# Two-layer attention backbone on one core: exponentials left unscaled, gates divided by the row sums, and another order of the first loads

## The chip, the cores and the metric

One core of one Trainium2 chip runs the whole program in one launch. The metric is device time in microseconds (us); less is better. Engines are named as in the profile: PE (matrix multiply, with PEld its weight loads), DVE (vector), ACT (scalar), POOL (GpSimd), SP (issues the DMAs).

## The reference

Two layers over 512 latent tokens (a grid of 8 rows and 64 columns) and 256 context tokens, width 1024. Cut to what matters:

```python
hx = _rmsnorm(x, norm_g) * (1.0 + scale_x) + shift_x       # scale, shift from silu(c) @ w_ada + b_ada
px = hx @ w_in                                              # one projection for everything below
a_k, a_v, b_k, b_v, a_q, b_q, a_z, b_z, g_a, g_b = _split(px, SPLIT_SIZES)
# branch A: 8 heads, neighbourhood window 8 x 16 with a bias, and all context keys
# branch B: 8 query heads on 2 key heads, rotary, all latent and all context keys
p = jax.nn.softmax(s, axis=-1)
a_att = p @ v                                               # the same for b_att
o_a = (a_att * jax.nn.silu(a_z)) @ w_o_a
o_b = (b_att * jax.nn.silu(b_z)) @ w_o_b
merged = jax.nn.sigmoid(g_a) * o_a + jax.nn.sigmoid(g_b) * o_b
x_new = x + gate_x * (merged @ w_out)
```

In layer 0 the context tokens go through the same computation (they read context keys alone); in layer 1 only the latent tokens are updated. All is float32.

## The kernel before

**Products.** Every float32 operand of a product is split into a high and a low part, and each product is three matmuls (`mm3`: high by high, high by low, low by high; lines 345 to 347). Weights come by `load_w` and `load_w2`: a DMA into one of three `raw` tiles, ACT writes the high part `whi` (lines 315, 330), DVE or POOL the low part `wlo` (lines 318, 332).

**Stages of a layer.** The projections for branch A (keys, values, queries); the attention of branch A, called NA below (`na_scores`, `na_values`); the projections for branch B; the attention of branch B, called GQ (`gq_scores`, `gq_values`); then the merge: the two output projections, the sigmoid gates, `w_out` and the residual. The gate projections (`fill_chunks`, `o_chunks`) are cut into pieces and handed out between heads as filler for PE (`run(fill, ...)`).

**One head of attention.** `pipeline` takes the scores of head h, and then the values of head h-1. For each of four blocks of 128 queries PE puts the scores in PSUM, DVE finds the row maximum (line 753 in NA, 899 in GQ), and ACT takes the exponential into a tile `p` with the row sums in `r` (lines 756, 901). Then `softmax_tail` takes the reciprocal of the sums on DVE (line 607) and multiplies `p` with 0.5 and the reciprocal: in blocks 0 and 2 on DVE (line 610), in blocks 1 and 3 on POOL (lines 612 and 613). In layer 0 the context queries are a fifth block (`ctx_scores`, on DVE). The values transpose `p` on PE (lines 621, 623), split it (`pth` on ACT, line 626; `ptl` on DVE, line 627), multiply it with the values, and `head_out` (lines 635 to 637) adds two halves and multiplies the result into the gate tensor `za` or `zb`, which holds z times (1 + tanh(z/2)); the 0.5 makes that silu. The `p` tiles come from a pool of 7 slots in NA of layer 0, 8 in NA of layer 1, and 10 in GQ (`NP_NA`, `NP_GQ`). At the end of GQ `hilo` (lines 519, 520) splits `zb` for the output projection.

**The start of layer 0.** Six tiles of 128 tokens are loaded (`load_x`, line 130); the latent ones are gathered from the grid so that tokens run down the columns:

```python
x_lat = x0.rearrange("(r c) d -> c r d", c=GRID_W)
```

`start_y` normalises a tile and transposes it into `yT`. The modulation's weights come in four parts of 2 MB (`ada_load`: two DMAs `rawx` and `rawy`), each of which serves two of the eight channel blocks k; `ada_part` multiplies them with silu(c) on PE (line 190) and DVE makes scale and shift in `modc` (lines 171 to 173). `start_mods(q)` applies them to two channel blocks of `yT` (line 301), and ACT and DVE or POOL split the result into `hx` (lines 304, 305). Then the first projection (`C_AK`) takes these two blocks for all six token tiles, and so on for q = 0 to 3.

**Order.** The instructions are written in program order and then put in an order per engine by a planner with a model of the times (`schedule_with_timeline_sim=True`); each engine then runs its own list in that order, SP's DMA queue included.

Of the kernel before, what the change touches and what calls it, by code (L numbers as in the profile page):

```python
# [28 lines left out]
NA_POOL = (1, 3)  # L29
GQ_POOL = (1, 3)  # L30
# [17 lines left out]
def hybrid_kernel(es: ExitStack, tc, x, ctx, cvec, w_ada, w_ada0, small, gvec, w_in, w_o_a, w_o_b, w_out,  # L48
# [48 lines left out]

    x0, ctx0 = x[0], ctx[0]
    x_lat = x0.rearrange("(r c) d -> c r d", c=GRID_W)
# [33 lines left out]
    for t in range(6):  # L133
        load_x(t)
# [66 lines left out]
    def ada_steps(l, tiles, halves, nv, pool):  # L201
# [13 lines left out]
        def dot(h, i, v):  # L215
            if v == 0:
                load_tile(h, i)
            w = cb["w"]
            o = w if v == nv - 1 else pool.tile([128, 512], BF16, tag="junk", name=nm("junk"), bufs=1)
            ins = nc.cur_bb.bb.instructions  # L220
            before = next(j for j in reversed(ins) if j.engine == mybir.EngineType.DVE)
            n = len(ins)
            V.tensor_tensor_reduce(o, w, cb[h][:, v, :], 1.0, 0.0, ALU.mult, ALU.add, asum[:, i, h, v:v + 1])
            for j in nc.cur_bb.bb.instructions[n:]:
                if j.engine == mybir.EngineType.DVE:
                    tc.add_manual_dep(j, before.name, mybir.DependencyInfo(
                        mybir.DependencyClass.NoSync, mybir.DependencyReason.DATA), reason="program order")
# [69 lines left out]
    def start_mod(k, yT, hx):  # L297

        d = yT[k // 4].rearrange("p (k n) -> p k n", k=4)[:, k % 4, :]
        for v, (n0, n1) in enumerate(((0, 512), (512, 768))):  # L300
            V.tensor_scalar(d[:, n0:n1], d[:, n0:n1], modc[:, 0, v, 8 + k:9 + k], modc[:, 0, v, k:k + 1],
                            ALU.mult, ALU.add)
        hi, lo = hx_k(hx, 0, k), hx_k(hx, 1, k)
        S.copy(R(hi), d)
        (G if k % 3 == 2 else V).tensor_tensor(R(lo), d, hi, ALU.subtract)
# [65 lines left out]
    def start_mods(q):  # L371
        for k in range(2 * q, 2 * q + 2):
            start_mod(k, yT, hx0)
# [83 lines left out]
    def layer(l, hx, nxt, mid):  # L457
# [146 lines left out]
        if True:  # L604
            def softmax_tail(p, n, r, pieces, eng=None):

                V.reciprocal(r, r)  # L607
                for i, (c0, c1) in enumerate(pieces):
                    if eng is None:
                        V.tensor_scalar(p[:, c0:c1], p[:, c0:c1], r[:, i:i + 1], 0.5, ALU.mult, ALU.mult)  # L610
                    else:
                        G.tensor_scalar(r[:, i:i + 1], r[:, i:i + 1], 0.5, None, ALU.mult)  # L612
                        G.tensor_tensor(p[:, c0:c1], p[:, c0:c1],  # L613
                                        r[:, i:i + 1].to_broadcast([128, c1 - c0]), ALU.mult)
# [63 lines left out]
            def ctx_scores(q, kh, kl):  # L678
# [8 lines left out]
                r = sp.tile([128, 2], F32, tag="r", name=nm("r"), bufs=8)  # L687
                for i in range(2):
                    S.activation(p[:, 256 * i:256 * i + 256], pss[:, 256 * i:256 * i + 256], AF.Exp,
                                 bias=mx[:, i:i + 1], accum_out=r[:, i:i + 1])  # L690
                softmax_tail(p, 512, r, [(0, 256), (256, 512)])
# [41 lines left out]
            def na_scores(h, q, kh, kl):  # L733
                load_bias(h)
                ps_ = []
                for i in range(4):
# [4 lines left out]
                    else:  # L741
# [7 lines left out]
                        for kk, b in ((kh, True), (kl, False)):  # L749
# [5 lines left out]
                    r = sp.tile([128, 2], F32, tag="r", name=nm("r"), bufs=8)  # L755
                    S.activation(p[:, :512], p[:, :512], AF.Exp, bias=mx[:, 0:1], scale=-1.0,
                                 accum_out=r[:, 0:1])
                    softmax_tail(p, 512, r[:, 0:1], [(0, 512)], G if i in NA_POOL else None)
# [33 lines left out]
            def pipeline(fill, spread, scores_of, values_of, last=None, bg=[]):  # L792
# [13 lines left out]
                run(bg, len(bg))  # L806
                values_of(7, prev)
# [4 lines left out]
            def na_first(h):  # L812
# [4 lines left out]
                ps_ = na_scores(h, q, kh, kl)  # L817
                return ps_, ctx_scores(q, kh, kl) if first else None
# [12 lines left out]
            pipeline(fill, 9, na_first, values_of(za, na_values), bg=bg)  # L831
# [59 lines left out]
            def gq_scores(q, kh, kl):  # L891
                ps_ = []
                for i in range(4):
# [6 lines left out]
                    r = sp.tile([128, 2], F32, tag="r", name=nm("r"), bufs=8)  # L900
                    S.activation(p, pss, AF.Exp, bias=mx[:, 0:1], accum_out=r[:, 0:1])
                    softmax_tail(p, 768, r[:, 0:1], [(0, 768)], G if i in GQ_POOL else None)
# [19 lines left out]
            def gq_first(h):  # L922
                kh, kl = gkt[h // 4]
                q = stage_q(qbv[:, h // 2, :], h % 2)
                ps_ = gq_scores(q, kh, kl)
                return ps_, ctx_scores(q, kh, kl) if first else None
# [11 lines left out]
            pipeline(fill, 8, gq_first, values_of(zb, gq_values), early, bg)  # L938
# [149 lines left out]
```

## Time and profile before

| | us |
|---|---|
| median of 3 runs (1182.45 to 1184.28) | 1183.07 |
| profiled execution, time | 1181.47 |
| profiled execution, span | 1179.7 |
| start of layer 0 up to the end of its first projection | about 73 |
| NA, layer 0 and layer 1 | 173.0 and 114.3 |
| GQ, layer 0 and layer 1 | 186.5 and 142.7 |
| share of the span that PE, PEld, DVE, ACT, POOL are busy | 96%, 80%, 69%, 49%, 43% |

The edges of the stages were read from the first and last instructions of their lines. A matmul in the timeline lasts longer than the distance to the next one, because they are pipelined; so PE's busy share counts an engine as full that could have run its matmuls more densely.

### The profile page before, as it was taken

The numbers are of one execution on the slowest core, as the hardware profiler recorded it, in microseconds if no ns is written. First come the engines' busy times: TensorE is split into PE (matmuls) and PEld (weight loads), VectorE is DVE, ScalarE is ACT, GpSimd is POOL, SyncE is SP. The second block draws the span as 40 slices with busy tenths as digits, with TensorE's granted clock in tenths as the row PEclk, the third lists the DMA queues.
The fourth block names the chain that finished last, engine by engine and source line by source line (L and its number), as shares of the span: only waits on it lengthen the run. The fifth ranks groups of instructions, "written<-read, shape, count | busy, mean of one in ns | idle before, by whom it ended". The sixth has DMA issues, their size and how long they took to land. (4 is left out here: it accounts for less than half of the span.)

```text
span 1179.7 us, 17337 instructions
## 1 busy us (share of the span) xinstructions
PE 1130.4 (96%) x6078; PEld 948.8 (80%) x6078; DVE 812.2 (69%) x1506; ACT 575.0 (49%) x1171; POOL 508.3 (43%) x463
## 2 busy tenths in 40 slices
PE   4999999899999999999999999999999999999898
PEld 3688877788897888878788887887888878877686
DVE  4476689987474499978683455339786757798573
ACT  4353255466453355566430355436666545756531
POOL 2362444453267233453420225336553764654311
PEclk9999999999999999999999999999999999999999
DMA  9544323422152343371170322312322525452133
GB/s 315 188 144 135 111 80 111 120 82 61 55 157 87 118 143 112 72 263 38 41 192 18 125 90 72 116 43 88 119 78 71 159 80 183 142 179 98 37 127 96
DMA packets 88128, 134.05 MB, mean 114 GB/s; under 512 B 10756, under 2 KB 52712, under 8 KB 86376
## 3 DMA queue, kind: packets, MB, share of 16 engines
q1 hardware_dynamic: 88040, 132.94, 36.1%
q8 instruction: 48, 0.79, 0.3%
q14 instruction: 40, 0.33, 0.1%
HBM read 115.58 MB, written 17.32 MB: 113 GB/s over the span
## 5 line engine op out<-in xcount | busy, mean ns | idle before, releaser
L627 DVE TENSOR_TENSOR ptl<-pst,pth 128x512 fp32r<-128x512 f32 (+1 forms) x176 | 115.9, 672 | 40.7 <-ACT pth L626 39.6
L332 POOL TENSOR_TENSOR wlo<-raw,whi 128x512 fp32r<-128x512 f32 x64 | 91.7, 1435 | 119.8 <-ACT whi L330 99.6
L345 PE MATMUL psf<-hx,whi 128*128 128x512 f32 (+1 forms) x368 | 138.9, 378 | 1.1 <-DVE za L480 1.0
L346 PE MATMUL psf<-hx,whi 128*128 128x512 f32 (+1 forms) x368 | 138.3, 376 | 0.0
L347 PE MATMUL psf<-hx,wlo 128*128 128x512 f32 (+1 forms) x368 | 137.9, 375 | 0.0
L626 ACT CAST pth<-pst 128x512 fp32r<-128x512 f32 (+1 forms) x176 | 98.8, 578 | 80.0 <-PE pst L623 56.2
L345 PE MATMUL psx<-whi,hx 128*128 128x512 f32 (+1 forms) x368 | 134.9, 374 | 0.0
L346 PE MATMUL psx<-wlo,hx 128*128 128x512 f32 (+1 forms) x368 | 134.4, 369 | 0.0
L347 PE MATMUL psx<-whi,hx 128*128 128x512 f32 (+1 forms) x368 | 133.4, 370 | 0.0
L318 POOL TENSOR_TENSOR wlo<-raw,whi 128x512 fp32r<-128x512 f32 (+1 forms) x52 | 68.1, 1310 | 146.1 <-ACT whi L315 123.6
L315 ACT CAST whi<-raw 128x512 fp32r<-128x512 f32 (+1 forms) x112 | 64.8, 591 | 111.2 <-PE psx L347 39.6
L330 ACT CAST whi<-raw 128x512 fp32r<-128x512 f32 x128 | 78.1, 621 | 56.2 <-DMA raw<-in_w_in_dram 41.0
L623 PE MATMUL pst<-ident,p 128*128 128x128 f32 x640 | 100.4, 273 | 3.6 <-POOL p L613 1.2
L623 PEld LDWEIGHTS pst<-ident,p 128*128 128x128 f32 x640 | 77.8, 140 | 16.8 <-POOL p L613 1.6
L613 POOL TENSOR_TENSOR p<-p,r 128x512 f32<-128x512 f32 (+1 forms) x64 | 86.6, 1353 | 5.2
L332 DVE TENSOR_TENSOR wlo<-raw,whi 128x512 fp32r<-128x512 f32 x64 | 63.4, 991 | 36.0 <-ACT whi L330 35.5
L612 POOL TENSOR_SCALAR r<-r 128x1 f32<-128x1 f32 x64 | 24.2, 378 | 135.9 <-DVE r L607 123.9
L345 PEld LDWEIGHTS psf<-hx,whi 128*128 128x128 f32 x368 | 69.5, 189 | 12.9 <-DVE za L480 1.7
L347 PEld LDWEIGHTS psx<-whi,hx 128*128 128x128 f32 x368 | 69.4, 189 | 12.0 <-issue 0.8
L345 PEld LDWEIGHTS psx<-whi,hx 128*128 128x128 f32 x368 | 70.0, 191 | 11.1
L346 PEld LDWEIGHTS psx<-wlo,hx 128*128 128x128 f32 x368 | 69.6, 189 | 11.3
L347 PEld LDWEIGHTS psf<-hx,wlo 128*128 128x128 f32 x368 | 69.4, 188 | 11.6
(239 smaller groups left out, 3049.4 us busy)
## 6 DMA issues: line engine op xcount, KB each, us to landing
raw<-in_w_in_dram SPq DMA_DIRECT2D x160, 256.0 KB, 2.9
rawb<-in_w_ada_dram SPq DMA_DIRECT2D x64, 256.0 KB, 2.7
gs<-zt SPq DMA_DIRECT2D x32, 256.0 KB, 2.6
raw<-in_w_out_dram SPq DMA_DIRECT2D x32, 256.0 KB, 2.7
tg<-gs SPq DMA_DIRECT2D x4, 1536.0 KB, 7.8
rawx<-in_w_ada_dram SPq DMA_DIRECT2D x4, 1024.0 KB, 11.9
rawy<-in_w_ada_dram SPq DMA_DIRECT2D x4, 1024.0 KB, 12.7
raw<-in_w_o_a_dram SPq DMA_DIRECT2D x16, 256.0 KB, 3.2
```

What stands on the lines that cost most here:

```text
L315: S.copy(hi[:, :n], raw[:, :n])
L318: e.tensor_tensor(lo[:, :n], raw[:, :n], F(hi[:, :n]), ALU.subtract)
L330: S.copy(hi, raw)
L332: lo_eng(i).tensor_tensor(lo, raw, F(hi), ALU.subtract)
L345: T.matmul(ps, lhs[0], rhs[0], start=first, stop=False)
L346: T.matmul(ps, lhs[0], rhs[1], start=False, stop=False)
L347: T.matmul(ps, lhs[1], rhs[0], start=False, stop=last)
L612: G.tensor_scalar(r[:, i:i + 1], r[:, i:i + 1], 0.5, None, ALU.mult)
L613: G.tensor_tensor(p[:, c0:c1], p[:, c0:c1], r[:, i:i + 1].to_broadcast([128, c1 - c0]), ALU.mult)
L623: T.transpose(pt[:, c0:c0 + 128], src, ident)
L626: S.copy(hi[:, n0:n1], pt[:, n0:n1])
L627: V.tensor_tensor(lo[:, n0:n1], pt[:, n0:n1], F(hi[:, n0:n1]), ALU.subtract)
```

## The change

The exponentials are no longer multiplied with anything. The sums of the two heads of a pair, for all query blocks, are kept in one tile `r` of 128 by 12 (8 in layer 1). `invert` doubles them and takes the reciprocal; `sums_out` transposes them on PE into 12 rows of 128, ACT copies these into a `p` tile, and a DMA writes them to DRAM. One head later `normalise` reads them back, each row to 64 partitions, into one or two `p` tiles, and POOL multiplies the pair's channels of `za` or `zb` with them. For the last pair this comes ahead of the values of head 7. `behind` fixes the place of some of these instructions: after what was written before them on the same engine.

At the start, only two token tiles are loaded ahead of the modulation's first part; then come the first two channel blocks of the projection's weights, the other four token tiles, and the modulation's second part. The first two token tiles are normalised ahead of `ada_part(0)`, the other four behind it. `start_mods(0)` works in groups of 256 tokens. The weights of the projection's next part are loaded ahead of the modulation's next part. The host lays x out in column order, so that each token tile is one contiguous piece of DRAM.

```diff
+    rd = [drp.tile([12, 128], F32, name=f"rd{i}") for i in range(4)]
...
         if t < 4:
-            return x_lat[16 * t:16 * t + 16]
+            return x0[128 * t:128 * t + 128, :]
...
-    for t in range(6):
+    for t in range(2):
         load_x(t)
...
-    def start_mod(k, yT, hx):
+    def start_mod(k, yT, hx, cuts):
         d = yT[k // 4].rearrange("p (k n) -> p k n", k=4)[:, k % 4, :]
-        for v, (n0, n1) in enumerate(((0, 512), (512, 768))):
-            V.tensor_scalar(d[:, n0:n1], d[:, n0:n1], modc[:, 0, v, 8 + k:9 + k], modc[:, 0, v, k:k + 1],
-                            ALU.mult, ALU.add)
         hi, lo = hx_k(hx, 0, k), hx_k(hx, 1, k)
-        S.copy(R(hi), d)
-        (G if k % 3 == 2 else V).tensor_tensor(R(lo), d, hi, ALU.subtract)
+        for n0, n1 in zip(cuts, cuts[1:]):
+            for v, (c0, c1) in enumerate(((n0, min(n1, 512)), (max(n0, 512), n1))):
+                if c0 < c1:
+                    V.tensor_scalar(d[:, c0:c1], d[:, c0:c1], modc[:, 0, v, 8 + k:9 + k], modc[:, 0, v, k:k + 1],
+                                    ALU.mult, ALU.add)
+            S.copy(R(hi[:, n0:n1]), d[:, n0:n1])
+            (G if k % 3 == 2 else V).tensor_tensor(R(lo[:, n0:n1]), d[:, n0:n1], hi[:, n0:n1], ALU.subtract)
...
     def start_mods(q):
-        for k in range(2 * q, 2 * q + 2):
-            start_mod(k, yT, hx0)
+        cuts = (0, 256, 512, 768) if q == 0 else (0, 768)
+        for i in range(len(cuts) - 1):
+            for k in range(2 * q, 2 * q + 2):
+                start_mod(k, yT, hx0, cuts[i:i + 2])
...
                 if q == 0:
-                    mid(0)
+                    mid(0, lambda: w.extend(load_w(W, C_AK, 512, 2, mix_lo)))
                 if q < 3:
-                    mid(q + 1)
+                    mid(q + 1, lambda: w.extend(load_w(W, C_AK, 512, 2, mix_lo, 2 * q + 2)))
                 start_mods(q)
-                w += load_w(W, C_AK, 512, 2, mix_lo, 2 * q)
...
+            def invert(r):
+                n = 6 if first else 4
+                V.tensor_scalar(r[:, 0:n], r[:, 0:n], 2.0, None, ALU.mult)
+                V.reciprocal(r[:, 0:n], r[:, 0:n])
+
+            def sums_out(j, r):
+                n = 12 if first else 8
+                pt = psw(128, "t")
+                T.transpose(pt[0:n], r[:, 0:n // 2].rearrange("p j e -> p (j e)"), ident)
+                row = p_tile()[:, 0:128]
+                S.copy(row[0:n], pt[0:n])
+                behind(lambda: nc.sync.dma_start(rd[j][0:n], row[0:n]))
+
+            def normalise(j, z, perm):
+                zv = z.rearrange("p (f n) -> p f n", f=4)[:, j]
+                n = 6 if first else 4
+                w = min(att["w"] // 128, n)
+                for j0 in range(0, n, w):
+                    j1 = min(j0 + w, n)
+                    rb = p_tile()[:, 0:128 * (j1 - j0)]
+                    for e in range(2):
+                        nc.sync.dma_start(rb[64 * e:64 * e + 64].rearrange("p (j q) -> p j q", q=128),
+                                          rd[j].rearrange("(j e) q -> e j q", e=2)[e:e + 1, j0:j1]
+                                          .to_broadcast([64, j1 - j0, 128]))
+                    if perm and j0 == 0:
+                        zp = zv[:, 0:512].rearrange("p (s n) -> p s n", n=64)[:, 0:8:7]
+                        G.tensor_tensor(zp, zp, rb[:, 0:128].rearrange("p (s n) -> p s n", n=64), ALU.mult)
+                        G.tensor_tensor(zv[:, 64:448], zv[:, 64:448], rb[:, 128:512], ALU.mult)
                     else:
-                        G.tensor_scalar(r[:, i:i + 1], r[:, i:i + 1], 0.5, None, ALU.mult)
-                        G.tensor_tensor(p[:, c0:c1], p[:, c0:c1],
-                                        r[:, i:i + 1].to_broadcast([128, c1 - c0]), ALU.mult)
+                        zp = zv[:, 128 * j0:128 * j1]
+                        G.tensor_tensor(zp, zp, rb, ALU.mult)
...
-                    softmax_tail(p, 512, r[:, 0:1], [(0, 512)], G if i in NA_POOL else None)
...
-                    softmax_tail(p, 768, r[:, 0:1], [(0, 768)], G if i in GQ_POOL else None)
...
                     if prev is not None:
                         values_of(h - 1, prev)
+                    if h % 2:
+                        invert(att["r"])
+                        sums_out(h // 2, att["r"])
+                    elif h:
+                        behind(lambda: normalise(h // 2 - 1, z, perm))
...
                 run(bg, len(bg))
+                normalise(3, z, perm)
                 values_of(7, prev)
...
-    def start_part(q):
+    def start_part(q, load):
         if q == 0:
             ada_w[0] = ada_load(0, npool)
-            for t in range(6):
+            load()
+            for t in range(2, 6):
+                load_x(t)
+            ada_w[1] = ada_load(1, npool)
+            for t in range(2):
                 start_y(t, npool, yT)
-        if q < 3:
-            ada_w[q + 1] = ada_load(q + 1, npool)
+        else:
+            load()
+            if q < 3:
+                ada_w[q + 1] = ada_load(q + 1, npool)
         ada_part(q, ada_w.pop(q), npool)
+        if q == 0:
+            for t in range(2, 6):
+                start_y(t, npool, yT)
...
+    d['x'] = d['x'].reshape(1, ROWS, GRID_W, DM).transpose(0, 2, 1, 3).reshape(1, NLAT, DM)
```

More of the change, by code (lines that the diff above doesn't have):

```diff
@@ L96, in psw, with behind @@
         return pool.tile([128, cols], F32, tag=kind, name=nm("ps" + kind))[:, :n]
+    def behind(fn):
+        ins = nc.cur_bb.bb.instructions
+        n, last = len(ins), {}
+        for i in ins[::-1]:
+            last.setdefault(i.engine, i.name)
+            if len(last) == 5:
+                break
+        fn()
+        for i in nc.cur_bb.bb.instructions[n:]:
+            if i.engine in last:
+                tc.add_manual_dep(i, last[i.engine], mybir.DependencyInfo(
+                    mybir.DependencyClass.NoSync, mybir.DependencyReason.DATA), reason="program order")
+            last[i.engine] = i.name
     x0, ctx0 = x[0], ctx[0]
-    x_lat = x0.rearrange("(r c) d -> c r d", c=GRID_W)
     o_lat = out[0].rearrange("(r c) d -> c r d", c=GRID_W)
@@ L219, in dot @@
             o = w if v == nv - 1 else pool.tile([128, 512], BF16, tag="junk", name=nm("junk"), bufs=1)
[L220 to L227, printed above, removed]
+            behind(lambda: V.tensor_tensor_reduce(o, w, cb[h][:, v, :], 1.0, 0.0, ALU.mult, ALU.add,
+                                                  asum[:, i, h, v:v + 1]))
         res = []
@@ L676, in cut, with ctx_scores @@
                 return lambda k: k[:, a:b]
-            def ctx_scores(q, kh, kl):
+            def ctx_scores(q, kh, kl, r, e):
                 pss = ps_score()
```

43 lines of the change are left out of this document (20 added, 23 removed).

## The prediction

> **What bounds the kernel now.** First the page's totals, then the busy time of each engine by stage. The stages, in order: start of layer 0; NA of layer 0; projections for branch B; GQ of layer 0; merge; and from layer 1 projections, NA, GQ. The columns are PE, PEld, DVE, ACT, POOL (instructions in brackets), clock, DMA share, GB/s.
>
> ```profile
> span 1179.7 us, 17337 instructions
> PE 1130.4 (96%) x6078; PEld 948.8 (80%) x6078; DVE 812.2 (69%) x1506; ACT 575.0 (49%) x1171; POOL 508.3 (43%) x463
> ...
> 0.00:73.00 73.00, 56.73 (x282) 40.23 (x283) 34.73 (x71) 32.04 (x54) 22.80 (x29) 0.98 0.69 236
> 158.50:331.50 173.00, 165.71 (x1038) 146.73 (x1039) 139.60 (x309) 95.68 (x220) 75.11 (x68) 1.00 0.30 91
> 331.50:404.50 73.00, 71.04 (x399) 61.00 (x399) 39.58 (x71) 29.43 (x65) 44.66 (x43) 1.00 0.38 116
> 404.50:591.00 186.50, 180.53 (x1092) 156.69 (x1091) 157.08 (x285) 106.50 (x222) 79.83 (x67) 1.00 0.37 112
> 591.00:718.00 127.00, 127.00 (x627) 107.26 (x626) 69.67 (x112) 45.69 (x101) 23.48 (x25) 1.00 0.32 97
> ...
> 800.70:915.00 114.30, 111.89 (x608) 94.60 (x607) 91.96 (x186) 72.59 (x155) 57.75 (x58) 1.00 0.29 89
> 971.30:1114.00 142.70, 137.31 (x703) 110.76 (x704) 113.72 (x198) 85.93 (x166) 68.80 (x59) 1.00 0.41 132
> ```
>
> PE is the bound. Outside the start it idles most in the four attention stages, where DVE is 80 to 84% busy (139.60 of 173.00, 157.08 of 186.50, 91.96 of 114.30, 113.72 of 142.70); where DVE is about half busy (39.58 of 73, 69.67 of 127) PE idles little or not at all. Idle in the four stages is only 7.3 + 6.0 + 2.4 + 5.4 = 21 us. But that understates what PE could save, as these rows of the timeline and of PE's groups in GQ of layer 1 show:
>
> ```profile
> 656.54 0.39 PE L346 MATMUL psx<-wlo,mh 128*128 128x512 f32 x1
> 656.77 0.39 PE L347 MATMUL psx<-whi,ml 128*128 128x512 f32 x1
> ...
> 1095.92 1.04 PE L623 MATMUL pst<-ident,p 128*128 128x128 f32 x8
> ...
> L623 PE MATMUL pst<-ident,p 128*128 128x128 f32 x192 | 29.1, 273 | 1.3 <-DVE ptl L627 1.2 <-POOL p L613 0.2
> L345 PE MATMUL psf<-hx,whi 128*128 128x512 f32 x56 | 22.2, 397 | 0.0
> ...
> L917 PE MATMUL psv<-ptl,vb 128*128 128x512 f32 x48 | 20.6, 429 | 1.0 <-DVE ptl L627 0.8
> ...
> L672 PE MATMUL pss<-gk,qs 128*128 128x512 f32 x32 | 14.1, 440 | 1.3 <-ACT p L901 0.9 <-DVE qs L666 0.3
> L345 PE MATMUL psf<-gah,whi 128*128 128x512 f32 x32 | 13.0, 405 | 0.3 <-DVE tg L554 0.3
> ...
> L672 PE MATMUL pss<-gk,qs 128*128 128x256 f32 x32 | 9.1, 284 | 0.0
> ```
>
> A 512-column matmul lasts 0.39 us but the next starts 0.23 later; eight transposes take 1.04, of which the last lasts 0.27, so 0.11 apart. At those distances the 703 matmuls of this stage need: 192 transposes, 21 us; 424 wide ones (three lines of 56 and of 32, two of 48 and of 32), at 0.227, 96 us; of the 87 left 64 are of 256 columns, counted half, 7 us, and 23 wide, 5 us. Sum 130 of 142.7: 13 us, 9%, is waiting, much of it hidden inside "busy". By the same share the four stages (616.5 us) hold about 55 us. A page of the Trainium skill says just this: "Perfetto Trace Analysis", section "Identifying the Most-Contended Engine", calls matmul busy time a bad measure of headroom because matmuls are pipelined. By busy time alone the attention's gain could not pass 21 us; the distances above bear the page out.
>
> **Part 1, the softmax.** What goes:
>
> ```profile
> L610 DVE TENSOR_SCALAR p<-p,r 128x512 f32<-128x512 f32 x32 | 24.3, 758 | 0.6
> L610 DVE TENSOR_SCALAR p<-p,r 128x768 f32<-128x768 f32 x32 | 23.7, 740 | 1.9 <-PE pst L623 0.5
> L607 DVE RECIPROCAL r<-r 128x1 f32<-128x1 f32 x128 | 19.3, 156 | 10.6 <-ACT p L901 5.4 <-ACT p L756 4.6
> L610 DVE TENSOR_SCALAR p<-p,r 128x256 f32<-128x256 f32 x32 | 16.4, 552 | 0.3
> ...
> L613 POOL TENSOR_TENSOR p<-p,r 128x768 f32<-128x768 f32 x32 | 51.2, 1602 | 2.5
> L613 POOL TENSOR_TENSOR p<-p,r 128x512 f32<-128x512 f32 x32 | 35.4, 1105 | 2.7
> L612 POOL TENSOR_SCALAR r<-r 128x1 f32<-128x1 f32 x64 | 24.2, 378 | 135.9 <-DVE r L607 123.9 <-ACT pth L626 9.4 <-PE pst L623 1.2
> ...
> gs<-zt SPq DMA_DIRECT2D x32, 256.0 KB, 2.6
> ...
> cb<-cd SPq DMA_DIRECT2D x10, 256.0 KB, 3.6
> ```
>
> DVE loses 24.3 + 23.7 + 19.3 + 16.4 = 84 us and 16 two-column reciprocals at about 0.16, 2.5: 86 us. It gains 16 pairs of two small operations, 32 x 0.16 = 5. Net 81 of the 502 us that DVE is busy in the four stages, 16%; 81% busy becomes 68%. POOL loses 51.2 + 35.4 + 24.2 = 111 us. Per pair it gains a product over 768 columns in layer 0 (1.6, in NA in three pieces, so 2.2) and over 512 in layer 1 (1.1, in NA in two, 1.5): about 26 us in all. PE gains 16 transposes of at most 0.1 each, and ACT 16 copies of 128 columns, bounded by 0.1 and by the 0.6 of a 512-column copy: under 10 us on an engine that is 49% busy.
>
> PE rarely waits for the scaled `p` itself: the rows name 0.5 and 0.2 us. The scaling costs as time on DVE's queue, ahead of `ptl`, of the row maxima and of the evacuations that PE does wait for, and as latency: blocks 1 and 3 stand 0.4 + 1.1 to 1.6 us on POOL after DVE. How much of 55 us this frees no row shows. Lower bound: the waiting shrinks as DVE's time does, 16%, 9 us. Upper bound: half of it, 27 us, because the other half lies at the stages' ends, where the last head's transposes, `pth` and `ptl` follow one another with nothing beside them, which the change leaves alone. I take the middle, **18 us**; both ends are kept. Below nothing is a rival.
>
> The round trip through DRAM: a store lands 2.6 us after issue, a broadcast load 3.6. For three pairs of four the load is written a head after the store (a head takes an eighth of its stage, 14 to 23 us), so nobody waits. What queues behind: SP's later loads of weights, bias and modulation rows, and POOL's low parts. The last pair is the exposed one. In GQ of layer 1:
>
> ```profile
> 1095.17 1.47 POOL L613 TENSOR_TENSOR p<-p,r 128x768 f32<-128x768 f32 x1
> ...
> 1112.57 1.29 POOL L637 TENSOR_TENSOR zb<-zb,ho 64x512 f32<-64x512 f32 x1 [6.04 <-DVE ho L636]
> ```
>
> The last scaling ends at 1096.6, the product that must now follow the pair's normalisation begins at 1112.6: 16 us of cover, with POOL idle for 6.04 at its end. The new chain is about 0.3 (DVE) + 1 (PE, ACT) + 2.6 + 3.6 + 1.1 = 9 us. Cost nothing; were the cover gone, 9 us in each layer, part of the slower rival.
>
> **Part 2, the start.** Rows of the timeline, and the DMA totals of 3 to 12 us (x from the grid) and of 14 to 38 us (all else):
>
> ```profile
> 2.05 2.59 SPq L130 DMA_DIRECT2D x<-in_x_dram  x4
> ...
> DMA packets 576, 2.02 MB, mean 224 GB/s; under 512 B 52, under 2 KB 88, under 8 KB 576
> ...
> DMA packets 1979, 10.12 MB, mean 422 GB/s; under 512 B 235, under 2 KB 251, under 8 KB 956
> ...
> 22.72 1.07 PE L190 MATMUL pst<-rawx,scol 128*32 128x512 f32 x8 [0.35 <-DVE yT L295]
> ...
> 27.50 1.65 DVE L301 TENSOR_SCALAR yT<-yT,modc 128x512 f32<-128x512 f32 x4
> ...
> 28.39 0.83 ACT L304 CAST hx<-yT 128x768 fp32r<-128x768 f32 x1 [2.58 <-DVE yT L301]
> ...
> 29.28 0.80 PE L345 MATMUL psf<-whi,hx 128*128 128x512 f32 x1 [2.28 <-ACT hx L304]
> 29.87 2.33 PE L345 MATMUL psx<-whi,hx 128*128 128x512 f32 x5
> ...
> 32.41 1.32 PE L346 MATMUL psx<-wlo,hx 128*128 128x512 f32 x5
> ```
>
> The modulation's first product (22.72) stands on PE behind the transposes of six tiles, and the first projection matmul comes 6.56 us after it. In the new order two token tiles (1.05 MB) and the first part (2.1 MB) at 422 GB/s take 7.5 us from about 3: landed at 10.5. With 1 us to see it, `L190` runs at 11.5, and the first projection matmul about 6 us later (the 256-token group shortens lines 301 and 304 from 0.8 each to some 0.4): 17.5 against 29.3, 12 us earlier. Not all is gain: the transposes of four tiles (32, some 0.13 each by the eight in 1.04, 4.2 us) and half of the second part's product (1.07) lay ahead of 29.28 and now lie behind: 12 - 5.3 = 6.7. The groups add four small instructions per channel block on DVE and ACT, beside PE. I take **6 us**, from 0 (see the cold start below) to 10 (if the pause from 24 to 29 and later ones close too).
>
> **Sum.** 1181.47 - 18 - 6 = 1157.5 for the profiled execution. Its span is 1179.7, with 1.8 around it, which stays. It lies 1.6 below the median of the runs, so **1159 us** against 1183.07. Less than 0.2%, 2.4 us, can hardly be told from no change.
>
> **Rivals.**
>
> *Only the start gains.* The waiting in attention comes from the order on PE's own queue and from PSUM slots. For it: PE's named waits for `p` are under 1 us. Against: stages with less DVE work have less of it. 1183 - 6 = 1177.
>
> *Cold start.* After the pause before 29.28 five matmuls took 2.33 us, a little later 1.32: 0.43 apart, then 0.23. The profile's granted clock is 0.98 over this stage. If q = 0 in three groups, with gaps until later tokens' `yT` come, stays at the slow pace for all its 36 matmuls, that costs 36 x 0.2 = 7 us and the start gains nothing: 1165. The Trainium skill, "TensorE: Matmul & The Clock Gate", Part 1, states such a rule: activity over a window of about 3.4 us releases the clock. By it two token tiles' work could be too sparse at first; the rows above agree with the slow pace after a pause.
>
> *More.* The waiting falls to half and the start gives 10: 1183 - 37 = 1146; 1140 if the stages' ends shorten a little too, since the last head's `p` comes 2 us earlier in each of them.
>
> *Slower: the `p` slots.*
>
> ```profile
> L753 DVE CUSTOM_DVE_ANT_0 p<-pss,bedg 128x512 f32<-128x512 f32 x16 | 11.0, 685 | 10.6 <-PE pst L623 9.3 <-PE pss L673 0.9 <-issue 0.4
> ```
>
> A head's first block already waits 9.3 us in all for transposes to free its `p`. Now the row and its broadcast copies sit in the same slots: 13 tiles a pair instead of 10 in NA of layer 0, the copies for 3.6 us of load and more on POOL's queue, longer when SP is held. If each of 16 pairs stalls PE by more than 24 / 16 = 1.5 us, the sum turns; at 2.5, 40 us are lost and the time is 1199. Against: a `p` no longer stays for reciprocal and scaling, some 2 us a block. Filler lies beside most heads.
>
> *Nothing moves.* The planner spends the freed time elsewhere: 1183.
>
> **How the numbers follow.** The forecast 0.55, only the start 0.12, cold start 0.10, more 0.09, slower 0.12, nothing 0.02. Faster 0.86, same 0.02, slower 0.12. The range is 1140 to 1183: it leaves out the slower rival and half of "more". The forecast's own range is 1148 to 1170.
>
> **What would show it.** Right: no lines 607, 610, 612, 613; DVE near 68% and PE with the same matmuls in shorter attention stages (18 us over four); the first projection matmul near 17.5 us and the start's end near 67 instead of 73; x packets at about 420 GB/s. Wrong: DVE's row maxima or exponentials waiting for transposes or for the broadcast load; `zb` at the end of GQ released by a DMA; SP idle in a long wait with `raw` loads late; the start's matmuls 0.43 apart; or stages as long as before at a lower DVE share.

## The result, and the profile after

The changed kernel takes 1184.66 us (median of 20 runs, 1183.10 to 1186.68), the kernel before 1183.10 (20 runs, 1180.19 to 1185.85): ratio 1.0015, interval 1.0009 to 1.0022. The forecast was 1159. First the totals of the page after:

```profile
span 1183.3 us, 17168 instructions
...
PE 1135.5 (96%) x6094; PEld 954.2 (81%) x6094; DVE 731.1 (62%) x1304; ACT 579.6 (49%) x1191; POOL 417.1 (35%) x363
```

DVE fell from 812.2 to 731.1, by the 81 us of the forecast; POOL fell by 91 where 85 were worked out. The work went as counted, and the time did not follow. By stage (start, NA and GQ of layer 0, NA and GQ of layer 1; columns as in the forecast's table):

```profile
0.00:73.00 73.00, 60.07 (x298) 43.69 (x299) 38.03 (x82) 35.28 (x64) 26.69 (x33) 0.95 0.68 250
153.90:321.20 167.30, 165.22 (x1038) 146.85 (x1039) 118.27 (x245) 97.20 (x223) 55.32 (x47) 1.00 0.33 104
...
396.70:580.20 183.50, 179.56 (x1096) 156.78 (x1095) 132.13 (x221) 107.21 (x226) 55.16 (x39) 1.00 0.38 122
...
789.60:907.20 117.60, 113.52 (x612) 96.13 (x611) 75.30 (x146) 73.90 (x159) 41.40 (x34) 0.99 0.31 96
...
964.60:1117.80 153.20, 142.18 (x707) 113.41 (x708) 98.59 (x158) 86.92 (x170) 40.89 (x31) 0.98 0.42 130
```

Layer 0 became shorter (173.0 to 167.3, 186.5 to 183.5), layer 1 longer (114.3 to 117.6, 142.7 to 153.2) while DVE's share there fell to 64%. In GQ of layer 1 DVE has 15 us less to do and the stage takes 10 us more.

To compare many kernels, the table takes one mark for all: an attention stage runs from DVE's first instruction of the row-maximum line (in NA that is a wait, which stands 4.3 us ahead of the maximum itself in layer 0 of the kernel before, and 2.3 in layer 1) to the start of its last product on POOL, a projection stage (P0, P1) from there to the next such mark. "Start" runs from zero to the first mark. Merge with the next layer's first projections took 211.6 to 211.9 in all, what follows GQ of layer 1 66.3 to 67.4. All in us, each row from one profiled execution, the last column the median of the runs.

| kernel | start | NA 0 | P0 | GQ 0 | NA 1 | P1 | GQ 1 | median |
|---|---|---|---|---|---|---|---|---|
| before | 155.1 | 176.2 | 74.3 | 184.2 | 113.3 | 57.2 | 140.3 | 1183.10 |
| changed | 150.5 | 170.7 | 76.6 | 181.2 | 116.6 | 58.4 | 150.8 | 1184.66 |
| start_only | 148.8 | 176.1 | 74.2 | 184.9 | 113.4 | 57.1 | 140.5 | 1177.45 |
| softmax_only | 153.5 | 170.8 | 73.9 | 181.2 | 115.6 | 57.4 | 150.3 | 1185.89 |
| layer0_only | 150.5 | 170.8 | 76.5 | 182.9 | 112.9 | 57.9 | 139.6 | 1169.56 |
| no_div | 149.0 | 172.1 | 75.6 | 181.1 | 112.9 | 56.7 | 143.5 | 1168.48 |
| ceiling | 149.8 | 171.7 | 75.6 | 181.1 | 112.9 | 57.3 | 139.1 | 1167.79 |
| dots_late | 148.8 | 170.7 | 76.3 | 181.2 | 116.7 | 58.4 | 144.0 | 1176.56 |
| dots_early | 147.9 | 177.8 | 74.2 | 185.0 | 113.3 | 56.8 | 144.4 | 1183.51 |
| own1 | 148.8 | 170.7 | 76.7 | 182.9 | 115.4 | 59.2 | 148.4 | 1182.66 |
| unpin | 149.0 | 170.1 | 74.1 | 181.6 | 115.6 | 57.4 | 151.8 | 1181.62 |
| sums_only | 148.7 | 170.8 | 76.6 | 183.4 | 114.8 | 58.4 | 149.6 | 1182.99 |
| reload_only | 149.3 | 170.7 | 76.5 | 183.0 | 113.2 | 58.3 | 140.5 | 1172.36 |
| sums_late | 148.9 | 170.8 | 77.0 | 181.2 | 115.2 | 59.2 | 144.7 | 1180.38 |
| direct1 | 150.5 | 170.8 | 76.8 | 181.2 | 126.1 | 56.8 | 155.2 | 1192.91 |
| all_fix | 148.9 | 170.1 | 74.1 | 181.2 | 115.4 | 58.5 | 149.2 | 1178.46 |
| dots_own | 148.6 | 170.7 | 76.2 | 182.7 | 116.2 | 58.5 | 146.7 | 1181.05 |
| layer0_unpin | 150.9 | 170.2 | 74.0 | 181.8 | 112.9 | 58.5 | 139.6 | 1167.45 |

GQ 0 shows how far one profile can be trusted: with the new softmax, and no edit between them in that stage, it took 181.2 to 183.4, although the instructions on PE, DVE, ACT and POOL stand there in the same order (changed against dots_late, own1, sums_only, sums_late and layer0_only). A difference of 2 us in one cell decides nothing; one that comes back in several rows does.

### The profile page after: what moved, and what is told of

Same layout as the page of the kernel before. It is cut to its first block, busy times and chain, and to the rows that moved or that the text cites. A ratio compares the mean times of both kernels' runs of the same rounds, so it can differ in the third digit from the quotient of the medians.

```text
span 1183.3 us, 17168 instructions
## 1 busy us (share of the span) xinstructions
PE 1135.5 (96%) x6094; PEld 954.2 (81%) x6094; DVE 731.1 (62%) x1304; ACT 579.6 (49%) x1191; POOL 417.1 (35%) x363
## 4 chain that ended last, share of the span: by engine, by line
PE 74%; DVE 9%; POOL 5%; DMA 4%; issue 3%; ACT 3%; SPq 0%; DVEq 0%; POOLq 0%; ACTq 0%
PE psx L354 10%; PE psx L355 10%; PE psx L356 10%; PE psf L354 8%; PE psf L355 8%; PE psf L356 8%; PE pst L660 4%; DMA raw<-in_w_in_dram 2%; PE pss L709 2%; PE pss L710 2%; PE pss L785 1%; PE psv L960 1%; DVE ptl L664 1%; PE psv L959 1%; PE pst L409 1%
## 5 line engine op out<-in xcount | busy, mean ns | idle before, releaser
L341 POOL TENSOR_TENSOR wlo<-raw,whi 128x512 fp32r<-128x512 f32 x64 | 88.8, 1390 | 202.5 <-ACT whi L339 168.3
L327 POOL TENSOR_TENSOR wlo<-raw,whi 128x512 fp32r<-128x512 f32 (+1 forms) x52 | 66.4, 1278 | 150.8 <-ACT whi L324 129.8
L341 DVE TENSOR_TENSOR wlo<-raw,whi 128x512 fp32r<-128x512 f32 x64 | 60.4, 944 | 53.0 <-ACT whi L339 52.5
L354 PEld LDWEIGHTS psf<-hx,whi 128*128 128x128 f32 x368 | 69.8, 190 | 19.3 <-ACT zt L489 5.4
L327 DVE TENSOR_TENSOR wlo<-raw,whi 128x512 fp32r<-128x512 f32 (+1 forms) x60 | 48.4, 811 | 50.8 <-ACT whi L324 50.1
L355 PEld LDWEIGHTS psf<-hx,whi 128*128 128x128 f32 x368 | 69.9, 190 | 10.4
## 6 DMA issues: line engine op xcount, KB each, us to landing
tg<-gs SPq DMA_DIRECT2D x4, 1536.0 KB, 10.1
```

The lines of the kernel that those rows point to most:

```text
L327: e.tensor_tensor(lo[:, :n], raw[:, :n], F(hi[:, :n]), ALU.subtract)
L341: lo_eng(i).tensor_tensor(lo, raw, F(hi), ALU.subtract)
L354: T.matmul(ps, lhs[0], rhs[0], start=first, stop=False)
L355: T.matmul(ps, lhs[0], rhs[1], start=False, stop=False)
```

## The experiments

### Which part, which layer

The kernels put back the old start, the old softmax, or the old softmax in layer 1 alone.

```diff
 start_only:    ROWS_OUT = (False, False)   # old softmax in both layers
 softmax_only:  start_part, start_mod, load_x and x's layout of before
 layer0_only:   ROWS_OUT = (True, False)    # new softmax in layer 0 only
```

> The new beginning of layer 0, with the softmax of before in both layers. In the profiled run of the changed kernel the first NA score of layer 0 came at 153.9 us instead of 158.5. Theory 'given back' (what a stage saves stays saved unless a later stage's order gets worse): 4.6 us less, 1178.5. Rival 'the plan takes it' (any earlier start reshuffles the later queues and the profit is gone by the end): 1181 to 1186, with the later stages' lengths changed by several us although nothing in them is edited.

> The new softmax in both layers, with the beginning of before. In the changed kernel layer 0 gained 6.4 us after its beginning and layer 1 lost 14.8. If the loss belongs to the new softmax of layer 1: 1183 - 6.4 + 14.8 = 1191. If it belongs to one order of the queues that comes out anew with each edit: layer 0 still gains 6 us, layer 1 lands anywhere between -8 and +15: 1169 to 1192, with other pauses in other places.

> The changed kernel, with the softmax of before in layer 1 alone. If the loss in layer 1 belongs to the new softmax there: layer 1 as before, layer 0 as changed, 1183 - 11 = 1172. If it belongs to an order that any edit shakes: the layer 1 stages differ from both kernels, 1172 to 1186.

Measured, with the ratio to the kernel before and its interval: 1177.45 (0.9955, 0.9942 to 0.9969), 1185.89 (1.0026, 1.0017 to 1.0035) and 1169.56 (0.9886, 0.9872 to 0.9899). The start gives 5.5 us and keeps them; the plan does not take them back. The new softmax lengthens GQ 1 by 10 us with the old start as well (150.3 beside 150.8), so it is no accident of one order. With the old softmax in layer 1, its stages are again those of before. The gain is in layer 0, the loss belongs to the new softmax in layer 1. The stages say so more than the times: softmax_only's 1185.89 misses the 1191 of that theory and lies in the wide range of the other, while layer0_only's 1169.56 is 2.4 under the theory's 1172 and outside the other's range.

### The division or the scaling

```diff
 no_div
-                    if h % 2:
-                        invert(att["r"])
-                        sums_out(h // 2, att["r"])
-                    elif h:
-                        behind(lambda: normalise(h // 2 - 1, z, perm))
...
-                normalise(3, z, perm)
 ceiling: no_div, and in gq_scores
-                    run(att["bg"], att["per"])
+                    if first or att["h"]:
+                        run(att["bg"], att["per"])
```

> The changed kernel without the division: no sums transposed, no rows to DRAM and back, no product on POOL, no row tiles in the p slots, nothing pinned on SP's queue; the output lacks the division by the sums. If the p slots or the round trip through SP give the gain back: at least 10 us under the changed kernel, 1174 or less. If the freed DVE and POOL time never was PE's wait, or if order and clock give it back: within 4 us of the changed kernel, 1181 to 1187.

> The changed kernel without the division (that part is left out), and with the modulation's products in GQ of layer 1 begun one head later: what the removed scaling is worth when nothing is paid for it. If the two costs add: 1168.5 - 7 = 1161.5, so that against 1177.45 of the new start alone the scaling is worth 16 us in four stages, near the 18 forecast. If they overlap: 1165 to 1169.

Measured: 1168.48 (0.9881, 0.9867 to 0.9894) and 1167.79 (0.9868, 0.9853 to 0.9883). The division costs 16 us by the medians, and in attention it costs in layer 1 alone: NA 1 and GQ 1 are 11.0 us shorter without it, NA 0 and GQ 0 are not. (no_div and ceiling leave the division out, so their output is incomplete.) And the scaling itself is worth less than forecast: from start_only to ceiling, where nothing is paid for its removal, the four stages give 4.4, 3.8, 0.5 and 1.4 us, 10.1 together, and the median 9.7. Layer 1 gives 1.9 of them. The 1161.5 expected from adding the two costs was missed by 6: without the division, the later products save 4.4 us in GQ 1 and 0.7 in the median, not 7, so the prices overlap: how much is put down to each depends on which is taken out first.

### The products that lost their spacer

Between the attention blocks run the modulation's products (`ada_steps`): weights `rawb` by DMA, one product on DVE (line 233) after each block, which `behind` places after the last DVE instruction written before it. That used to be the block's reciprocal or scaling, which wait for the exponential. Now it is the row maximum. Timeline of the changed kernel, first head of GQ 1:

```profile
965.58 0.96 DVE L944 TENSOR_REDUCE mx<-pss 128x1 f32<-128x768 f32 x1 [0.34 <-PE pss L710]
...
969.17 0.81 DVE L233 CUSTOM_DVE_ANT_0 rawb<-rawb,cb 128x512 f32<-128x512 f32 x1 [2.63 <-DMA rawb<-in_w_ada_dram]
...
969.91 0.94 DVE L944 TENSOR_REDUCE mx<-pss 128x1 f32<-128x768 f32 x1
970.02 1.80 SPq L226 DMA_DIRECT2D rawb<-in_w_ada_dram  x2
...
971.91 2.74 SPq L336 DMA_DIRECT2D raw<-in_w_in_dram  x3
...
976.44 0.62 ACT L339 CAST whi<-raw 128x512 fp32r<-128x512 f32 x1 [3.52 <-DMA raw<-in_w_in_dram]
976.97 0.59 ACT L489 ACTIVATE zt<-psf 128x512 f32<-128x512 f32 x1
...
977.61 0.80 PE L354 MATMUL psf<-hx,whi 128*128 128x512 f32 x1 [4.06 <-ACT zt L489]
```

and the same place in layer0_only, with the old softmax:

```profile
963.10 1.82 DVE L967 TENSOR_REDUCE mx<-pss 128x1 f32<-128x768 f32 x2 [0.34 <-PE pss L724]
...
966.75 0.88 DVE L234 CUSTOM_DVE_ANT_0 rawb<-rawb,cb 128x512 f32<-128x512 f32 x1 [0.82 <-DMA rawb<-in_w_ada_dram]
```

Read the first from its end: PE waits 4.06 us for ACT to free a PSUM bank (`zt`); ACT's `zt` stands behind a cast that waits 3.52 for weights; those weights were issued at 971.91, on SP behind two `rawb` loads that could not go before DVE had used the tiles; and DVE stood 2.63 us in front of a `rawb` that had not landed, with the second row maximum behind it. In the old order two maxima come first, and the product waits 0.82. Two kernels test it from both sides: the products begun one head later, and the old softmax with the products put ahead of the scaling.

```diff
 dots_late (changed kernel, gq_scores)
-                    run(att["bg"], att["per"])
+                    if first or att["h"]:
+                        run(att["bg"], att["per"])
 dots_early (start_only, GQ of layer 1)
+                    run(att["bg"], att["per"])
                     softmax_tail(p, 768, r2[:, 0:1], [(0, 768)], G if i in (1, 3) else None)
                     ps_.append(p)
-                    run(att["bg"], att["per"])
```

> The changed kernel; in GQ of layer 1 the products for the modulation (one after each block's row maximum) begin with the second head instead of the first. Theory 'the dot lost its spacer': with the scaling gone, the first product stands on DVE right behind the first row maximum, waits 2.63 us for its weights and holds the next maxima, and with them the tile order on SP and ACT; the pause of 4.2 us on PE near 973 goes, and so does the half-clock stretch behind it (1.7 us): 1184.7 - 5.9 = 1179. Rival 'raw weights are late on SP anyway': the pause stays or comes elsewhere, 1183 to 1187.

> The kernel with the new start and the old softmax (1177.45); in GQ of layer 1 the modulation's products now stand right behind each block's row maximum, ahead of its scaling, as the changed kernel has them. Nothing else differs. Theory 'the scaling was the spacer': the pause of about 4 us on PE appears in the first head of this GQ too, with no change to the softmax: 1181.5 to 1184. Rival 'the pause comes from the new softmax in another way': within 1.5 us of 1177.45.

Measured: dots_late 1176.56 (0.9938, 0.9923 to 0.9953), 8.1 under the changed kernel, GQ 1 6.8 shorter. dots_early 1183.51 (0.9994, 0.9977 to 1.0012), 6.1 over start_only, GQ 1 3.9 longer. Timeline of dots_early on DVE:

```profile
966.96 0.96 DVE L967 TENSOR_REDUCE mx<-pss 128x1 f32<-128x768 f32 x1 [0.34 <-PE pss L724]
970.65 0.72 DVE L234 CUSTOM_DVE_ANT_0 rawb<-rawb,cb 128x512 f32<-128x512 f32 x1 [2.73 <-DMA rawb<-in_w_ada_dram]
...
971.30 0.95 DVE L967 TENSOR_REDUCE mx<-pss 128x1 f32<-128x768 f32 x1
```

The same wait, 2.73 us, with every line of the old softmax in place: that the early products stall DVE and cost time without the new softmax is shown. The pause on PE is split there (1.14 and 1.38 us), not one of 4. What the stall costs depends on the rest of the queues. In no_div both waits stand as well:

```profile
963.10 0.69 DVE L233 CUSTOM_DVE_ANT_0 rawb<-rawb,cb 128x512 f32<-128x512 f32 x1 [3.11 <-DMA rawb<-in_w_ada_dram]
...
969.96 0.80 PE L354 MATMUL psf<-hx,whi 128*128 128x512 f32 x1 [2.97 <-ACT zt L489]
```

and there the later products of ceiling save 0.7 us of the median (3.4 between the two profiled runs), against 8.1 with the division; with the old softmax the early products cost 6.1.

### What the division costs in layer 1

```diff
 own1, layer 1:       row and rb in tiles of their own (tags "row", "rb", bufs=1) instead of p_tile()
 unpin:               behind(lambda: X) becomes X in sums_out and normalise
 sums_only, layer 1:  no normalise
 reload_only:         dots_late; layer 1 without invert and sums_out
 sums_late:           dots_late; layer 1 calls sums_out at h = 2, 4, 6 for the pair before, normalise at h = 3, 5, 7
 direct1:             dots_late; layer 1 without transpose, copy and row:
+    nc.sync.dma_start(rd[j][0:n].rearrange("n p -> p n"), r[:, 0:n // 2].rearrange("p j e -> p (j e)"))
```

> The changed kernel; in layer 1 the row and its broadcast copy have buffers of their own, so that the p slots are left to the exponentials. Leaving out the division gave 7 us in GQ of layer 1 and 4 in NA. If the p slots are what it costs: most of these 11 us, 1174 to 1178. If it is the chain or the place in the queues: within 2 us of 1184.7.

> The changed kernel without the fixed place of the row's store, the reloads and the products on their queues. If the fixed place costs (SP's weight loads or POOL's low parts stand behind it): 5 us or more under 1184.7. If not: within 2 us of 1184.7.

> The changed kernel; in layer 1 the sums are still transposed, copied and stored, but not loaded back, and no product divides by them there (that part of the computation is left out). If the reload on SP's queue and the products on POOL cost the 11 us in layer 1: 1174 to 1176. If the transposes and the row copies, which stand on PE's and ACT's queues ahead of exponentials, cost them: 1182 to 1185.

> The changed kernel with the products begun one head later (1176.6); in layer 1 no sums are inverted, transposed, copied or stored (that part is left out), but the reloads and the products stay and take what layer 0 left in DRAM. If the sending side costs: NA of layer 1 near 113 and GQ near 140, together 6 to 8 us less, 1169 to 1171. If the receiving side costs: within 2 us of 1176.6.

> The changed kernel with the products begun one head later (1176.6); in layer 1 a pair's sums are transposed and sent one head later, when their exponentials are long done, and reloaded one head later; the last pair as before. If the sending side costs because it stands on PE and ACT ahead of work that is ready: at least 4 us less, 1172 or under. If not: within 2 us of 1176.6.

> The changed kernel with the products begun one head later (1176.6); in layer 1 the inverted sums go from their own tile straight to DRAM in four-byte pieces, with no transpose on PE, no copy on ACT and no row in a p slot. If these steps cost: NA of layer 1 near 113.2 and GQ near 140.5, as without sending at all, 1169 to 1171. If the dependence or the store itself costs: 1175 to 1179, and the last pair's product on POOL may wait for a slower store.

Against the changed kernel's 1184.66: own1 1182.66, unpin 1181.62, sums_only 1182.99. So the p slots are worth 2 us, the receiving side (reload, product) 1.7, both short of the 7 to 11 that they were to explain. unpin's 3.0, between its two expected values, lies outside attention: P0 takes 74.1 instead of 76.6. Three kernels with the transposes and no fixed places have 74.0 or 74.1 there, nine with the new start and fixed places 76.2 to 77.0; softmax_only has 73.9 with fixed places and the old start, so it takes both to lose the 2.5. Against dots_late's 1176.56: reload_only 1172.36, NA 1 at 113.2 and GQ 1 at 140.5. The sending side (transpose, copy, row, store) holds 7.0 of the 8.7 us between dots_late and ceiling in these two stages; in the median, which falls between the two expected values, 4.2 of it are seen, and GQ 0, where nothing was edited, is 1.8 us longer in its profile. reload_only also spares the reload its wait for the store, but that is not the price: sums_only, which sends and reloads nothing, still holds 8.0 of the 11.0 us between the changed kernel and no_div in these stages. sums_late, which sends a head later, took 1180.38, 3.8 more than dots_late, outside both expected values; its profile shows the two stages 0.8 shorter, so the stages don't explain the median, but the 4 us that the place in the queue was to be worth did not come back.

What the sending does shows in where the filler ends up. Matmuls of line 345 (before) and 354 (changed, then the last row of ceiling) in NA 1, heads 0 to 5 and then, from the first row maximum of head 6, heads 6 and 7; columns PE, PEld, clock, DMA share, GB/s:

```profile
804.00:886.10 82.10, 30.79 (x79) 14.65 (x78) 1.00 0.32 100
886.10:916.40 30.30, 8.25 (x26) 4.94 (x26) 1.00 0.21 66
```

```profile
792.90:882.60 89.70, 34.49 (x88) 16.37 (x87) 1.00 0.34 105
882.60:908.40 25.80, 4.62 (x16) 3.16 (x17) 0.93 0.25 73
```

```profile
872.20:904.10 31.90, 8.99 (x28) 5.31 (x28) 1.00 0.21 63
```

The amount is the same (105 and 104, a third of the filler), but the last two heads keep 16 instead of 26. In ceiling they keep 28, in reload_only 28. Added up over the timeline's distances between matmuls, as far as they exceed 0.227 us (512 columns), 0.119 (256) or 0.109 (128), PE waits 7.0 us in the last head of NA 1 (first row maximum to last product) instead of 4.1. That filler moved ahead together with the sending is shown. That this movement alone makes the 7 us is not: own1, sums_late and dots_own keep 21, 22 and 24 there, sums_only 17, yet NA 1 takes 115.4, 115.2 and 116.2 in the first three and 114.8 in the last.

direct1 was to remove transpose, copy and row and keep the rest. It took 1192.91 (1.0089, 1.0063 to 1.0116), far over both expected values. The packets of the DMA queue in the changed kernel, then the same row and the new store (KB each, us to landing) in direct1, and two waits of its NA 1:

```profile
q1 hardware_dynamic: 99240, 138.26, 36.5%
```

```profile
q1 hardware_dynamic: 107432, 138.26, 38.4%
...
rd<-r SPq DMA_DIRECT2D x8, 4.0 KB, 10.3
```

```profile
POOL za L650 <- DMA p<-rd: 10.1, 1, 10.1
ACT whi L339 <- DMA raw<-in_w_in_dram: 9.3, 2, 6.2
```

A store of 4 KB in four-byte pieces lands 10.3 us after issue. The eight of them add 8192 packets, 1024 each, and the reload and the weight loads are late. The Trainium skill, "DMA: Bandwidth & Descriptors", section "Rules for kernel authors", says that a non-contiguous last dimension becomes one descriptor per element; the packet count agrees. The question was not answered this way: a wait that I added hid the one that I meant to remove. direct_all and direct_l0 used the same store in both layers and in layer 0:

> The changed kernel with three edits: products begun one head later in GQ of layer 1, sums straight to DRAM in both layers, no fixed places on SP and POOL. If the steps of the sending cost and the projections of layer 0 gain 2.5 without fixed places: 1167 to 1169. If not: 1173 to 1177.

> New start, new softmax in layer 0 alone, no fixed places, sums straight to DRAM. The attention of layer 0 took as long with the division as without it, so the sending costs nothing there: 1166 to 1169, against 1167.5 with the transposes.

Measured: 1212.28 (1.0241, 1.0224 to 1.0258) and 1191.08 (1.0069, 1.0048 to 1.0089). In direct_l0 the eight stores of layer 0, 6 KB each, land 10.5 us after issue, and by the marks of the table NA 0 and GQ 0 take 180.8 and 194.2 instead of the 170.2 and 181.8 of layer0_unpin.

### Edits together

```diff
 all_fix:       dots_late + own1 + unpin
 dots_own:      dots_late + own1
 layer0_unpin:  layer0_only + unpin
```

> The changed kernel with three edits: products begun one head later (GQ of layer 1), own buffers for row and copies in layer 1, no fixed places on SP and POOL. If the gains add (8.1, 2.0 and 3.0): 1171.6. If what the division costs is neither slots nor fixed places: no lower than 1173.

> The changed kernel with the products begun one head later and own buffers for row and copies in layer 1. If the two gains are prices that add: GQ of layer 1 near 141.6 and NA near 115.4, 1173. If each edit makes a new order of the queues with a cost of its own: GQ near 149 as in the kernel with all three edits, 1177 to 1180.

> New start, new softmax in layer 0 alone, and no fixed places on SP and POOL. Without the fixed places the projections of layer 0 took 74.1 instead of 76.6 us. If that is theirs: 1169.6 - 2.5 = 1167. If it was one plan among others: 1168 to 1172.

Measured: 1178.46 (0.9966, 0.9952 to 0.9980), 1181.05 (0.9979, 0.9968 to 0.9990) and 1167.45 (0.9869, 0.9854 to 0.9883). The last is the best complete kernel found, 1.3% under before; against layer0_only the intervals overlap. all_fix stayed above 1173, as expected if the division costs neither slots nor fixed places; dots_own missed both of its expected values in GQ 1 and in the median. Both show that the gains do not add: GQ 1, with the products begun later, takes 144.0, with own buffers as well 146.7, and 149.2 without the fixed places too. Timeline of all_fix:

```profile
1060.62 0.62 ACT L339 CAST whi<-raw 128x512 fp32r<-128x512 f32 x1 [5.57 <-PE psf L356]
1061.15 0.89 ACT L947 ACTIVATE p<-pss,mx 128x768 f32<-128x768 f32 x1
...
1062.18 0.50 PE L710 MATMUL pss<-gk,qs 128*128 128x512 f32 x1 [1.64 <-ACT p L947]
```

ACT stands 5.57 us in front of a cast whose buffer PE still uses, and the exponential that PE needs for its next scores is behind it. So an edit that takes one wait away can bring another order of the queues, with waits of its own.

## Why the prediction was wrong, point by point

The start held in size. Three steps failed: the middle of two bounds as the worth of the scaling (18 forecast, 9.7 measured), a round trip at no cost (8.8), and the removal of DVE work taken as time alone, with no term for the products that lost their place (8.1). By the medians, the sum that was forecast as -6, -18 and 0 came out as follows.

| term | forecast | measured | from |
|---|---|---|---|
| start | -6 | -5.5 | start_only against before |
| scaling gone | -18 | -9.7 | ceiling against start_only |
| division, round trip | 0 | +8.8 | dots_late against ceiling |
| products without their spacer | not seen | +8.1 | changed against dots_late |
| sum | -24 | +1.7 | changed against before: +1.6 |

The last two rows depend on the order of taking out: by way of no_div the division is 16.2 and the products 0.7. Their sum, 16.9, does not.

**The start: right in size, wrong in its working.** The first row is the modulation's product, on PE at 12.72:

```profile
12.72 1.94 PE L203 MATMUL pst<-rawx,scol 128*32 128x512 f32 x8
...
16.35 0.66 PE L208 MATMUL pst<-ident,row 128*128 128x128 f32 x4 [0.72 <-ACT row L205]
19.92 1.94 PE L300 MATMUL pst<-ident,x 128*128 128x128 f32 x8 [2.91 <-DVE x L296]
21.52 0.78 PE L354 MATMUL psf<-whi,hx 128*128 128x512 f32 x1
22.09 0.63 PE L355 MATMUL psf<-wlo,hx 128*128 128x512 f32 x1
22.52 0.63 PE L354 MATMUL psx<-whi,hx 128*128 128x512 f32 x1
```

It was to come at 11.5 and the first projection matmul 6 us later; it came 8.8 later, at 21.52, because PE's order put transposes of later tiles ahead (19.92), which wait for DVE. The first matmuls are 0.43 apart, as the cold-start rival said, at a granted clock of 0.50 from 18.2 to 25.0 us; from 25.06 on they are 0.23 apart, so not for all 36.

**Scaling: the step that failed first.** The waiting was counted rightly. By the same distances the four stages of before, from first row maximum to last product, hold 16.1, 16.0, 7.4 and 16.1 us, 56 in all against the 55 taken. The gain came out at the lower bound, 9 us, that the forecast had worked out from DVE's share of 16%; no row had spoken for the middle. And one share was applied to all four stages. In the last head alone lie 1.7, 4.9, 4.1 and 9.0: 13.1 of layer 1's 23.5. "Half lies at the stages' ends" was true of layer 1 and was averaged over a layer 0 where it is 6.6 of 32.1. In ceiling the last heads still hold 1.5, 4.9, 4.1 and 8.9, so the ends gave almost nothing back. The removed scaling shortened the stages of layer 0 by 8.2 and those of layer 1 by 1.9.

**The round trip: right where it was looked at.** In the last pair of GQ 1:

```profile
1109.00 1.28 POOL L674 TENSOR_TENSOR zb<-zb,ho 64x512 f32<-64x512 f32 x1 [4.02 <-DVE ho L673]
1111.03 1.28 POOL L651 TENSOR_TENSOR zb<-zb,p 128x512 f32<-128x512 f32 x1 [0.75 <-DMA p<-rd]
1116.38 1.28 POOL L674 TENSOR_TENSOR zb<-zb,ho 64x512 f32<-64x512 f32 x1 [4.07 <-DVE ho L673]
```

The product waits 0.75 for the reload and is done 4.07 before POOL's next one can begin: the chain is covered, as worked out. The price stands elsewhere, in the sending of every pair of layer 1 (7.0 us by reload_only), which the forecast had costed at "at most 0.1" per transpose and under 10 us of ACT's free time. Engine time was the wrong measure for a step that stands on PE and ACT between a head's last exponential and the next head; by which path it costs, beyond the filler that moves, stays open.

**The products: not in the forecast at all.** The diff shows `behind` around the product, and the old code did the same. What was not asked is what stands in front of a pinned instruction once the line in front of it is gone. This is the step "DVE loses 86 us", taken as time only: the removed operations also kept the product away from the maximum.

**Rivals.** "The p slots" ended on the right side and was the wrong mechanism: own buffers in layer 1 gave back 2 us of the 16 that the division costs. "Nothing moves" gave the right time, at a chance of 0.02, by a mechanism that the runs refute: the start's gain and layer 0's stayed to the end. Two losses in layer 1 happen to equal two gains before it; that is luck. The chance of a gain, 0.86, was too high because cover was looked for on one chain alone, the last pair's round trip, and not at the steps that every pair adds or at the instructions behind the removed ones.

## What to carry to other kernels

Before an operation is removed from an in-order queue, ask what is placed after it and what it kept apart: a product pinned behind the scaling cost 8.1 us when only the row maximum was left in front of it, and 0.7 where the division was left out as well. Take waiting apart by stage and by head before giving it a share: of the 13.1 us in the last heads of layer 1, 13.0 still stood when DVE had less to do. Try a change that touches several stages in each of them: with the new start, the new softmax in layer 0 alone and without fixed places is 1.3% faster than before, in both layers as changed 0.15% slower.

## What the runs showed of the hardware

Three stretches of half clock stand in layer 1 of the changed kernel, none in that of before. Windows, with busy PE and the granted clock; first the 3.4 us before each stretch, for PE alone, then the stretches:

```profile
892.00:895.40 3.40, 1.45 (x11) 1.00 0.00 0
973.90:977.30 3.40, 0.00 (x0) 1.00 0.65 195
1096.80:1100.20 3.40, 1.68 (x8) 1.00 0.00 0
```

```profile
895.40:898.80 3.40, 3.20 (x11) 2.71 (x12) 2.19 (x5) 1.06 (x4) 2.68 (x3) 0.50 0.00 0
977.30:980.80 3.50, 3.19 (x8) 2.55 (x9) 3.47 (x8) 2.39 (x5) 0.00 (x0) 0.51 0.58 168
1100.20:1103.60 3.40, 3.20 (x12) 2.73 (x12) 1.21 (x3) 1.09 (x2) 0.50 (x1) 0.50 0.00 0
```

Each is 3.4 us long at 0.50 and so costs, by an estimate, about 1.7 us, 5 in all. The Trainium skill, "TensorE: Matmul & The Clock Gate", Part 1, gives an idle window of about 3.4 us as what takes the clock away. The middle row agrees. The outer rows do not: there PE was busy for 1.45 and 1.68 of the 3.4 us, and the longest waits that the timeline names are 1.41 and 1.29 us. A short pause can cost its own length again. But it need not. In NA 0 of the kernel before, PE's wait is longer than those two, and the granted clock stays at 1.00 behind it:

```profile
232.05 0.33 PE L621 MATMUL pst<-ident,p 128*128 128x128 f32 x1 [3.27 <-DVE ptl L627]
```

So the length of a wait does not by itself tell which one costs clock.
